# Two-layer streaming trunk: longer runs of equal products, both output projections in half blocks, one engine swap and a block of gates moved

## The chip, the cores and the metric

The kernel runs on one core of one Trainium2 chip. The time is device microseconds of one execution; the kernel before has a median of 1018.46 us over three runs (1017.2 to 1019.1). All durations inside the kernel are from the trace of one profiled execution.

## The reference

A batch of one, 256 frames, model width 2048, two layers, each h = h + Mixer(RMSNorm(h)), in float32. Cut to what matters:

```python
# layer A: gated delta rule, 16 heads of 128, chunks of 64 frames
proj = h @ w_in                                   # 2048 x 8224: q, k, v, z, a, b
qkv = silu(causal_depthwise_conv(proj[..., :6144], conv_w))
q, k = l2_norm(q) * 128 ** -0.5, l2_norm(k)
gc = cumsum(-exp(a_log) * softplus(a + dt_bias)); decay = exp(where(tril, gc_i - gc_j, -inf))
u, w = triangular_solve(I + tril(k_beta @ k.T * decay, -1), [v_beta, k_beta * exp(gc)])
# scan over the chunks: v_new = u - w @ state; o = q_dec @ state + (q k.T * decay) @ v_new
y = (rms_norm(o, out_norm_w) * silu(z)) @ w_out   # 2048 x 2048

# layer B: attention in a band of 9 chunks, 16 heads of 128
proj = h @ w_in                                   # 2048 x 8192: q, k, v, z
p = softmax(rms_norm(q) @ rms_norm(k).T * 128 ** -0.5 + bias[rel])
y = ((p @ v) * silu(z)) @ w_out                   # 2048 x 2048
```

## The kernel before, in words

Nearly all of TensorE's work is the four big projections. Their weights come from HBM in 320 chunks of 512 KB (tile `wt`, four buffers), each once. For each chunk ScalarE rounds it to a high part (`whi`, L199) and VectorE takes the rest as a low part (`wlo`, L200). The activations are split in the same way (`xb`, or `g` for the output projections, with an axis of two for the high and the low part), and a product is high x high + high x low + low x high. The sums are gathered in PSUM in tiles named `psp`; the small matmuls of the mixers use tiles named `pss`.

A chunk is used in one of three forms (`KINDS`, L260).
- features (L234): 512 weight columns, two k-tiles of 128 rows. Four times per k-tile three products of 256 columns: L237, L239, L240.
- half (L242): 256 weight columns, four k-tiles. For a k-tile and one of two column groups there is one long product of 512 columns (the high weights by both parts of the activations, L247) and one short one of 256 (the low weights by the high part, L250): a pair. Four long ones are followed by four short ones (`GROUP` = 2 k-tiles by 2 column groups). When such a block is done, its two sums are joined by a copy on ScalarE (L303) and an addition on VectorE (L304).
- tokens (L253): the activations are the stationary side; three products of 512 columns: L256, L257, L258.

`plan` lists the chunks in order. A full block is 8 chunks in the features or the tokens form (`CPB`), 4 in the half form (`CPH`). Behind the products of each k-tile, `chunk` calls `step`, which advances one of two queues of background work (`bgq`, `bg2`), generators that emit a piece at each `yield`. That is how the convolutions, the decays, the inversion, the recurrence and the attention get in between the products. The order in which the program is written so is then arranged per engine, and each engine works through its instructions in that order.

The places that the change touches:
- `decays` (L455 to L492). For four groups of heads, right-hand sides are written (`rhs`, L457; the high part on VectorE, the low part on GpSimd, L460), TensorE sums them with constant triangular and all-one matrices (L475), and ScalarE takes exponentials (L480, L481, L483).
- `inversion` (L596). ScalarE first gathers blocks in eight copies (L610); VectorE transposes them (L620); later there are 64 matmuls of 32x32 (L650), and more of that size (L670).
- The end of layer A's recurrence, for the last four heads: the last products L780 to L782, squares on ScalarE (L783), their sum on VectorE (L789, L790), a power on GpSimd (L792), the scaling (L798) and the gates (L714) on VectorE; then `gated(3)` (L812) transposes the result on TensorE (L818) and writes it in two parts (L822, L823). The output projection's products for the k-tiles 12 to 15 need it: `ready` (L726) steps the queues until it has been emitted, and `drain` emits all that is left.
- Layer A's output projection starts before that. Its first 1024 columns are two features accumulators. Six of the eight chunks of each (`CUT`, the k-tiles 0 to 11) come first, then a drain, then the last two of each. The other columns are four half blocks. `ha_small` (L857) adds the input, whose rows GpSimd's queue fetches (L869), and splits the result for layer B.
- Layer B's input projection computes the gates z first (four pairs of half blocks; `zb_small`, which also asks for the bias rows), then v, then k and q for four groups of heads. `attend` has four stages: scores, weights (exponentials, L1023), turned (transposes L1037, copied by ScalarE in L1039) and values (L1047, L1048), behind which the gates are multiplied on. The last projection is cut like that of layer A.

## Time and profile before

| | |
|---|---|
| median of three runs | 1018.46 us |
| profiled execution, its time | 1018.52 us |
| its span | 1016.8 us |
| TensorE (PE) busy | 1005.7 us, 99% |
| VectorE (DVE) busy | 695.4 us, 68% |
| ScalarE (ACT) busy | 523.0 us, 51% |
| GpSimd (POOL) busy | 80.0 us, 8% |
| share of TensorE in the chain of waits | 95% |
| DMA | 177.56 MB, mean 175 GB/s |

In the rows of the profile an instruction stands with its line, its engine, its operation, its output and inputs by tile name, its shape and a count. PEld is TensorE's loading of the stationary side. A bracket gives the idle time of the engine ahead of the instruction, and who ended it. A matmul's duration reaches into the next one, so that the pace is the distance between starts. The view by windows gives, for a stretch, the busy time of each engine with a count of instructions, the granted clock of TensorE as a share of full speed, the DMA share and the rate.

### The profile page before, as it was taken

The numbers are of one execution on the slowest core, as the hardware profiler recorded it, in microseconds if no ns is written. First come the engines' busy times: TensorE is split into PE (matmuls) and PEld (weight loads), VectorE is DVE, ScalarE is ACT, GpSimd is POOL, SyncE is SP. The second block draws the span as 40 slices with busy tenths as digits, with TensorE's granted clock in tenths as the row PEclk, the third lists the DMA queues.
The fourth block names the chain that finished last, engine by engine and source line by source line (L and its number), as shares of the span: only waits on it lengthen the run. The fifth ranks groups of instructions, "written<-read, shape, count | busy, mean of one in ns | idle before, by whom it ended". The sixth has DMA issues, their size and how long they took to land.

```text
span 1016.8 us, 15574 instructions
## 1 busy us (share of the span) xinstructions
PE 1005.7 (99%) x6090; PEld 879.1 (86%) x6090; DVE 695.4 (68%) x1113; ACT 523.0 (51%) x724; POOL 80.0 (8%) x91
## 2 busy tenths in 40 slices
PE   8999999999999999999999999999999999999998
PEld 7987888888788989899988888888888888889987
DVE  7888889996988687755866555444456665666554
ACT  8475765555446455444654444444445555555442
POOL 2004000113000001001000000000011010101000
PEclk9999999999999999999999999999999999999999
DMA  8664665554664445545756766666665555544472
GB/s 289 183 187 115 178 184 155 156 166 146 185 190 144 108 142 149 163 145 168 246 187 187 228 207 207 188 195 196 189 186 177 153 169 163 165 154 159 158 228 90
DMA packets 134185, 177.56 MB, mean 175 GB/s; under 512 B 7904, under 2 KB 90208, under 8 KB 134112
## 3 DMA queue, kind: packets, MB, share of 16 engines
q1 hardware_dynamic: 132672, 172.12, 56.8%
q0 software_dynamic: 1152, 4.19, 1.2%
q8 instruction: 47, 0.77, 0.3%
q10 hardware_dynamic: 288, 0.26, 0.1%
q14 instruction: 26, 0.21, 0.1%
HBM read 174.46 MB, written 2.10 MB: 174 GB/s over the span
## 4 chain that ended last, share of the span: by engine, by line
PE 95%; DVE 2%; ACT 1%; issue 1%; DMA 1%; SPq 0%; ACTq 0%
PE psp L247 26%; PE psp L250 13%; PE psp L257 11%; PE psp L258 11%; PE psp L256 11%; PE psp L240 4%; PE psp L237 4%; PE psp L239 4%; PE pss L560 2%; DVE wlo L200 1%; PE pss L757 1%; PE pss L992 1%; PE pss L1011 1%; PE pss L1047 1%; PE pss L247 1%
## 5 line engine op out<-in xcount | busy, mean ns | idle before, releaser
L200 DVE TENSOR_TENSOR wlo<-wt,whi 128x1024 fp32r<-128x1024 f32 (+1 forms) x322 | 393.9, 1225 | 246.3 <-ACT whi L199 237.1
L199 ACT CAST whi<-wt 128x1024 fp32r<-128x1024 f32 (+1 forms) x322 | 336.4, 1046 | 399.3 <-PE psp L247 155.8
L247 PE MATMUL psp<-xb,whi 128*128 128x512 f32 x960 | 267.3, 397 | 0.3 <-DVE ev L304 0.3
L257 PE MATMUL psp<-wlo,xb 128*128 128x512 f32 x512 | 201.3, 393 | 1.6 <-DVE wlo L200 1.6
L258 PE MATMUL psp<-whi,xb 128*128 128x512 f32 x512 | 201.7, 394 | 0.0
L256 PE MATMUL psp<-whi,xb 128*128 128x512 f32 x512 | 200.3, 391 | 0.0
L247 PEld LDWEIGHTS psp<-xb,whi 128*128 128x128 f32 x960 | 165.1, 190 | 22.2 <-PE psp L250 0.5
L250 PEld LDWEIGHTS psp<-xb,wlo 128*128 128x128 f32 x960 | 147.9, 190 | 19.7
L250 PE MATMUL psp<-xb,wlo 128*128 128x256 f32 x960 | 156.7, 283 | 0.0
L257 PEld LDWEIGHTS psp<-wlo,xb 128*128 128x128 f32 x512 | 96.2, 188 | 21.6 <-DVE wlo L200 2.0
L256 PEld LDWEIGHTS psp<-whi,xb 128*128 128x128 f32 x512 | 96.2, 188 | 19.9 <-ACT whi L199 0.3
L258 PEld LDWEIGHTS psp<-whi,xb 128*128 128x128 f32 x512 | 96.3, 188 | 19.1
L239 PE MATMUL psp<-g,whi 128*128 128x256 f32 x256 | 73.5, 287 | 0.0
L237 PE MATMUL psp<-g,whi 128*128 128x256 f32 x256 | 73.5, 287 | 0.0
L240 PE MATMUL psp<-g,wlo 128*128 128x256 f32 x256 | 72.9, 285 | 0.0
L503 DVE SCALAR_TENSOR_TENSOR cv<-raw,sm,cv 128x254 f32<-128x254 f32 (+2 forms) x144 | 62.1, 477 | 1.8 <-ACT cv L501 1.8
L247 PE MATMUL psp<-g,whi 128*128 128x512 f32 x224 | 61.2, 395 | 0.0
L239 PEld LDWEIGHTS psp<-g,whi 128*128 128x128 f32 x256 | 49.1, 192 | 0.2
L237 PEld LDWEIGHTS psp<-g,whi 128*128 128x128 f32 x256 | 49.1, 192 | 0.1
L240 PEld LDWEIGHTS psp<-g,wlo 128*128 128x128 f32 x256 | 49.1, 192 | 0.1
L247 PEld LDWEIGHTS psp<-g,whi 128*128 128x128 f32 x224 | 38.3, 189 | 5.1
L250 PEld LDWEIGHTS psp<-g,wlo 128*128 128x128 f32 x224 | 34.4, 189 | 4.7
(248 smaller groups left out, 995.3 us busy)
## 6 DMA issues: line engine op xcount, KB each, us to landing
wt<-in_b_w_in_dram SPq DMA_DIRECT2D x128, 512.0 KB, 3.7
wt<-in_a_w_in_dram SPq DMA_DIRECT2D x127, 512.0 KB, 3.9
wt<-in_a_w_out_dram SPq DMA_DIRECT2D x32, 512.0 KB, 3.9
wt<-in_b_w_out_dram SPq DMA_DIRECT2D x32, 512.0 KB, 3.6
dl<-in_xT_dram POOLq DMA_DIRECT2D x4, 512.0 KB, 5.7
dl<-in_relb_dram POOLq DMA_DIRECT2D x4, 512.0 KB, 5.3
g<-in_xT_dram SPq DMA_DIRECT2D x7, 256.0 KB, 5.2
out_dram<-cv SPq DMA_DIRECT2D x2, 512.0 KB, 3.7
```

The costliest lines, as they stand in the source:

```text
L199: act.copy(out=hi[:, js, cs], in_=wt[:, js, cs])
L200: dve.tensor_tensor(out=lo[:, js, cs], in0=wt[:, js, cs], in1=hi[:, js, cs].bitcast(F32), op=ALU.subtract)
L237: pe.matmul(ps, lhsT=hi[:, j, fs], rhs=xb[:, kt, 0, :], start=(kt == 0 and s % 2 == 0), stop=False, skip_group_check=True)
L239: pe.matmul(ps, lhsT=hi[:, j, fs], rhs=xb[:, kt, 1, :], start=False, stop=False, skip_group_check=True)
L240: pe.matmul(ps, lhsT=lo[:, j, fs], rhs=xb[:, kt, 0, :], start=False, stop=(kt == KT - 1), skip_group_check=True)
L247: pe.matmul(ps[s], lhsT=hi[:, j, s * P:(s + 1) * P], rhs=xb[:, ks[j], :, :], start=(ks[j] == 0), stop=False, skip_group_check=True)
L250: pe.matmul(ps[s][:, 0, :], lhsT=lo[:, j, s * P:(s + 1) * P], rhs=xb[:, ks[j], 0, :], start=False, stop=(ks[j] == KT - 1), skip_group_chec ...
L256: pe.matmul(ps, lhsT=xh, rhs=hi[:, j, :], start=(kt == 0), stop=False)
L257: pe.matmul(ps, lhsT=xh, rhs=lo[:, j, :], start=False, stop=False)
L258: pe.matmul(ps, lhsT=xl, rhs=hi[:, j, :], start=False, stop=(kt == KT - 1))
L503: dve.scalar_tensor_tensor(out=cv[:, i, s:], in0=raw[:, i, :T - s], scalar=conv_w(i0 + i, 3 - s), in1=cv[:, i, s:], op0=ALU.mult, op1=ALU.add)
L560: pe.matmul(dst, lhsT=kq[:, a, i, c:c + P], rhs=rhs, start=(n == 0), stop=(n == 2))
```

## The change

- In the half form a whole chunk is one group: eight long products (four k-tiles by two column groups), then eight short ones. Odd chunks start with the short ones, so that where two chunks meet, sixteen of a kind follow each other.
- Background work is advanced in smaller portions: `tick` counts a credit, in the tokens form after each of the two halves of a k-tile. The inversion yields more often. The third block of layer A's gates has the rate 2, not 1.
- The decays' low parts are written by ScalarE: 32 copies of 128x128 with a scale in place of eight products on GpSimd.
- Both output projections have eight half blocks. The first part is now two half blocks with three of four chunks each.
- In layer B the last group's gates (256 x 2 columns) are computed behind the last queries. The last four heads' attention results are kept (`late`) and gated when these gates are there (`late_gates`). The fourth request for bias rows goes behind the values' first block.

```diff
-    CUT = (3 * CPB) // 4
     CUTH = (3 * CPH) // 4
 
-    def cut_halves(w, col):
+    def cut_halves(w, col, n=6):
 
         p = []
         for c0, c1 in ((0, CUTH), (CUTH, CPH)):
             for j in range(2):
                 p += half(w, col + 256 * j, c0, c1)
-        return p + halves(w, col + 512, 6)
-
-    for c0, c1 in ((0, CUT), (CUT, CPB)):
-        for j in range(2):
-            plan += wide(a_w_out, 512 * j, c0, c1)
-    plan += halves(a_w_out, 1024, 4)
-    plan += cut_halves(b_w_in, 6144)
+        return p + halves(w, col + 512, n)
+
+    plan += cut_halves(a_w_out, 0)
+
+    plan += cut_halves(b_w_in, 6144, 4)
     for gi in range(4):
         plan += wide(b_w_in, 4096 + 512 * gi)
     for gi in range(4):
         for col in (2048, 0):
             plan += wide(b_w_in, col + 512 * gi)
-    for c0, c1 in ((0, CUT), (CUT, CPB)):
-        for j in range(2):
-            plan += wide(b_w_out, 512 * j, c0, c1)
-    plan += halves(b_w_out, 1024, 4)
+    plan += halves(b_w_in, 7680, 2)
+    plan += cut_halves(b_w_out, 0)
...
+    credit = [0.0]
+
+    def tick(n):
+
+        while now:
+            now.pop(0)()
+        credit[0] += n
+        while credit[0] >= 1:
+            credit[0] -= 1
+            step()
...
+    def features2(ps, hi, lo, ks, xb):
+
+
+        turns = (ks[0] // len(ks)) % 2
+        for n, long in enumerate((not turns, turns)):
+            for s in range(2):
+                for j, kt in enumerate(ks):
+                    w = (hi if long else lo)[:, j, s * P:(s + 1) * P]
+                    dst, x = (ps[s], xb[:, kt, :, :]) if long else (ps[s][:, 0, :], xb[:, kt, 0, :])
+                    pe.matmul(dst, lhsT=w, rhs=x, start=bool(long and kt == 0), stop=(n == 1 and kt == KT - 1),
+                              skip_group_check=True)
+                yield
...
         if kind == "half":
             ps = ps if isinstance(ps, list) else [ps[:, s] for s in range(2)]
-            for j in range(0, kc, GROUP):
-                js = range(j, j + GROUP)
-                if pre is not None:
-                    for jj in js:
-                        pre(ks[jj])
-                features2(ps, hi, lo, js, ks, xb)
-                step(rate)
+            if pre is not None:
+                pre(ks[-1])
+            for _ in features2(ps, hi, lo, ks, xb):
+                tick(rate / 2)
             return
         for j, kt in enumerate(ks):
             if pre is not None:
                 pre(kt)
             for s in range(ns):
                 f(ps[:, s], s, j, kt, hi, lo, xb)
-            step(rate)
+                tick(rate / ns)
...
-                for part, src in ((0, g_r), (1, gl_r)):
-                    (pool if part else dve).tensor_tensor(
-                        out=rbuf[:, gi % 2, 2 * half + part, :].rearrange("p (h c) -> p h c", h=4),
-                        in0=lt_f.unsqueeze(1).broadcast_to([P, 4, P]),
-                        in1=src[:, 4 * gi:4 * gi + 4, half].bitcast(F32).unsqueeze(2).broadcast_to([P, 4, P]),
-                        op=ALU.mult)
+                dve.tensor_tensor(
+                    out=rbuf[:, gi % 2, 2 * half, :].rearrange("p (h c) -> p h c", h=4),
+                    in0=lt_f.unsqueeze(1).broadcast_to([P, 4, P]),
+                    in1=g_r[:, 4 * gi:4 * gi + 4, half].bitcast(F32).unsqueeze(2).broadcast_to([P, 4, P]),
+                    op=ALU.mult)
+                for i in range(4):
+                    act.activation(out=rbuf[:, gi % 2, 2 * half + 1, i * P:(i + 1) * P], in_=lt_f, func=AF.Copy,
+                                   scale=gl_r[:, 4 * gi + i, half:half + 1].bitcast(F32))
...
                 act.copy(
                     out=stg[pr].rearrange("p (h t) c -> p h t c", t=2)[:, :, t, :],
                     in_=dl[pr, :, 0, T * t + 32 * b:T * t + 32 * b + 32])
-            yield 1
+                yield 1
...
+                if i == 7:
+                    yield 1
...
+                if i % 4 == 3 and i < 15:
+                    yield 1
...
-        bg2.append(za_small(gi, block("tokens", xb, 1 if gi == 2 else 2)))
+        bg2.append(za_small(gi, block("tokens", xb, 2)))
...
-
-    pa = [acc("features") for _ in range(2)]
-    for n in (CUT, CPB - CUT):
+    pa = [acc("half") for _ in range(2)]
+    for n in (CUTH, CPH - CUTH):
         for j in range(2):
-            if n != CUT and j == 0:
+            if n != CUTH and j == 0:
                 drain()
             for _ in range(n):
-                chunk("features", pa[j], gmem["b"], 2, ready(gmem))
-            if n != CUT:
-                a_done(j, pa[j], 4 * j, 4 * j + 4)
-    for j in range(4):
-        a_done(j + 2, block("half", gmem["b"], 2), 8 + 2 * j, 10 + 2 * j)
+                chunk("half", pa[j], gmem["b"], 2, ready(gmem))
+            if n != CUTH:
+                bgq.append(ha_small(pa[j], slice(2 * j, 2 * j + 2)))
+    for j in range(2, 8):
+        bgq.append(ha_small(block("half", gmem["b"], 2), slice(2 * j, 2 * j + 2)))
...
-    for j in (1, 2, 3):
+    for j in (1, 2):
...
+            if gi == 3:
+
+                act.copy(out=late[:, i, :], in_=ps[:, :T])
+                return
...
+    late = hmem["m"][:, 8192:9216].rearrange("p (h t) -> p h t", h=4)
+
+    def late_gates():
+        for i in range(0, 4, 2):
+            o, hs = late[:, i:i + 2, :], slice(12 + i, 14 + i)
+            dve.tensor_tensor(out=o, in0=o, in1=bmem["z"][:, hs, :], op=ALU.mult)
+            act.copy(out=gmem["h"][:, hs, :], in_=o)
+            dve.tensor_tensor(out=gmem["l"][:, hs, :], in0=o, in1=gmem["h"][:, hs, :].bitcast(F32), op=ALU.subtract)
+            gmem["done"] = 14 + i
             yield 1
...
+    bgq.append(zb_small(3, pair(xb)))
+    bgq.append(late_gates())
...
-    po = [acc("features") for _ in range(2)]
-    for n in (CUT, CPB - CUT):
+    po, evs = [acc("half") for _ in range(2)], [[], []]
+    for n in (CUTH, CPH - CUTH):
         for j in range(2):
-            if n != CUT and j == 0:
+            if n != CUTH and j == 0:
                 drain()
             for _ in range(n):
-                chunk("features", po[j], gmem["b"], 1, ready(gmem))
-            if n != CUT:
-                bgq.append(out_small(j, po[j]))
-    for n in range(4, 7):
+                chunk("half", po[j], gmem["b"], 1, ready(gmem))
+            if n != CUTH:
+                joined(po[j], evs[j])
+                bgq.append(out_half(j, evs[j]))
```

How this moves instructions is shown at three places, as each engine's order has them. The lines of the changed kernel are a little further on in each function than before.

ScalarE, at the start of the decays. Before, up to the second group's exponentials:

```order
L199 CAST whi<-wt 128x1024 x3
L480 ACT_TABLE_LOAD
L480 ACTIVATE dl<-pss 128x4x128
L483 ACTIVATE dl<-pss,tail 128x128 x4
L481 ACTIVATE dl<-pss 128x4x128
L199 CAST whi<-wt 128x1024
L303 COPY ev<-psp 128x512
L480 ACTIVATE dl<-pss 128x4x128
```

Now (L468 writes a low part, L485, L486 and L488 are the exponentials, L193 the cast, L306 the copy of an eviction):

```order
L193 CAST whi<-wt 128x1024 x2
L468 ACTIVATE tt<-kT,gl_r 128x128 x16
L193 CAST whi<-wt 128x1024
L468 ACTIVATE tt<-kT,gl_r 128x128 x4
L485 ACT_TABLE_LOAD
L485 ACTIVATE dl<-pss 128x4x128
L193 CAST whi<-wt 128x1024
L306 COPY ev<-psp 128x512
L488 ACTIVATE dl<-pss,tail 128x128 x4
L486 ACTIVATE dl<-pss 128x4x128
L468 ACTIVATE tt<-kT,gl_r 128x128 x4
L193 CAST whi<-wt 128x1024
```

Twenty copies stand ahead of the first exponential, the other twelve between the later ones.

TensorE, at the end of layer A's recurrence. Before, the last products of the recurrence, and the first transposes of the last gates behind 76 products of the output projection:

```order
L782 MATMUL pss<-dl 128x128
L239 MATMUL psp<-g,whi 128x256
L240 MATMUL psp<-g,wlo 128x256
L237 MATMUL psp<-g,whi 128x256
...
L239 MATMUL psp<-g,whi 128x256
L818 MATMUL pss<-ident,dl 128x128 x2
```

Now (L789 to L791 are the recurrence's last products, L827 the transposes, L255 both kinds of product in the half form):

```order
L255 MATMUL psp<-g,wlo 128x256 x2
L791 MATMUL pss<-dl 128x128
L789 MATMUL pss<-dl 128x128
L790 MATMUL pss<-dl 128x128
L791 MATMUL pss<-dl 128x128 x2
L789 MATMUL pss<-dl 128x128
L790 MATMUL pss<-dl 128x128
L791 MATMUL pss<-dl 128x128
L827 MATMUL pss<-ident,dl 128x128 x8
L255 MATMUL psp<-g,wlo 128x256 x16
```

The transposes follow the recurrence's last product at once.

TensorE, at the end of the last attention. Before, 25 products stood between the transposes of a head's weights and its product with the values:

```order
L1037 MATMUL pss<-ident,raw 128x128 x3
L240 MATMUL psp<-g,wlo 128x256
L237 MATMUL psp<-g,whi 128x256
...
L240 MATMUL psp<-g,wlo 128x256
L1047 MATMUL pss<-pT,kT 128x256
L1048 MATMUL pss<-pT,kT 128x128
```

Now (L1046 are the transposes, L1056 and L1057 the products with the values):

```order
L255 MATMUL psp<-g,wlo 128x256 x8
L1056 MATMUL pss<-pT,kT 128x256
L1057 MATMUL pss<-pT,kT 128x128
L1046 MATMUL pss<-ident,raw 128x128 x3
L1056 MATMUL pss<-pT,kT 128x256
L1057 MATMUL pss<-pT,kT 128x128
L255 MATMUL psp<-g,whi 128x512 x8
```

The last head's product with the values follows its transposes at once.

More of the change, by code (lines that the diff above doesn't have):

```diff
@@ L217, in tile_hybrid_trunk, with step @@
     turn = [0]
-    def step(n=1):
+    def step():
         while now:
             now.pop(0)()
-        for _ in range(n):
-            lanes = (bgq, bg2) if turn[0] else (bg2, bgq)
-            turn[0] ^= 1
-            for lane in lanes:
-                if advance(lane):
-                    break
+        lanes = (bgq, bg2) if turn[0] else (bg2, bgq)
+        turn[0] ^= 1
+        for lane in lanes:
+            if advance(lane):
+                break
+    credit = [0.0]
[6 more added lines that the diff above has]
+            step()
     def drain():
@@ L869, in ha_small @@
             nc.gpsimd.dma_start(out=hmem["h"][:, qs, :], in_=xv[:, qs, :])
[L870 to L873 removed]
+        ev = work.tile([P, 2, T], F32, name="ev", tag="ev")
+        act.copy(out=ev, in_=ps[:, :, 1, :])
         yield 1
[L875 to L880 removed]
+        if k0 in (0, 4):
+            dve.tensor_copy(out=hmem["h"][0:1, k0 + 8, 0:1], in_=ev[0:1, 0, 0:1])
+        dve.tensor_tensor(out=h, in0=ps[:, :, 0, :], in1=h, op=ALU.add)
+        dve.tensor_tensor(out=h, in0=h, in1=ev, op=ALU.add)
         yield 1
@@ L936, in zb_small, with bias_load @@
         yield 1
+    def bias_load(gi, after):
+        bias, hs = bmem["bias"], slice(4 * gi, 4 * gi + 4)
+        dve.tensor_copy(out=bias[0:1, 4 * gi, 0:1], in_=after)
+        nc.gpsimd.dma_start(out=bias[:, hs, :], in_=relb[:, hs, :])
+        pool.memset(bias[0:64, hs, 192:256], NEG)
     while "x" not in hmem:
```

40 lines of the change are left out of this document (8 added, 32 removed).

## The prediction

> **What bounds the kernel now.** The busy times and the chain of waits come first.
>
> ```profile
> span 1016.8 us, 15574 instructions
> PE 1005.7 (99%) x6090; PEld 879.1 (86%) x6090; DVE 695.4 (68%) x1113; ACT 523.0 (51%) x724; POOL 80.0 (8%) x91
> PE 95%; DVE 2%; ACT 1%; issue 1%; DMA 1%; SPq 0%; ACTq 0%
> ```
>
> TensorE is busy for 99% of the span and carries 95% of the chain. A change can therefore save time in two ways only: by fewer or shorter matmuls, or by removing one of TensorE's few waits. Work added to ScalarE or VectorE costs nothing until TensorE waits for it. The waits of TensorE are the next view (total, times, longest):
>
> ```profile
> PE pss L475 <- ACT dl L480: 1.8, 1, 1.8
> PE psp L257 <- DVE wlo L200: 1.6, 1, 1.6
> PE psp L240 <- DVE wlo L200: 1.0, 2, 0.8
> PE pss L670 <- issue: 0.7, 1, 0.7
> PE psp L247 <- DVE ev L304: 0.3, 1, 0.3
> ```
>
> These five sum to 5.4 us, and none of them lies in layer A's output projection or in layer B (the L240 one is at the start). So what can be won is small, and any new wait is a loss of its full length. The third view is the pace of the products, in TensorE's timeline:
>
> ```profile
> 300.04 1.09 PE L247 MATMUL psp<-xb,whi 128*128 128x512 f32 x4
> 300.97 0.63 PE L250 MATMUL psp<-xb,wlo 128*128 128x256 f32 x4
> 305.65 0.63 PE L247 MATMUL psp<-xb,whi 128*128 128x512 f32 x2
> ...
> 640.02 0.39 PE L256 MATMUL psp<-whi,xb 128*128 128x512 f32 x1
> 643.88 0.39 PE L258 MATMUL psp<-whi,xb 128*128 128x512 f32 x1
> ...
> 471.29 0.28 PE L239 MATMUL psp<-g,whi 128*128 128x256 f32 x1
> 474.53 0.28 PE L239 MATMUL psp<-g,whi 128*128 128x256 f32 x1
> ```
>
> The duration of a matmul overlaps the next one, so starts are compared. In half blocks, four rounds of four long and four short products take 305.65 - 300.04 = 5.61 us, which is 351 ns for a pair of one long and one short. The first four long ones of a round take 0.93 us, 232 ns each, and the short ones the rest, 118 ns each. Long products without short ones between (17 from 640.02 to 643.88) come every 227 ns. Products of 256 columns in the features form (27 from 471.29 to 474.53) come every 120 ns, and a pair's worth is three of them: 360 ns.
>
> **The products (edits one and two).** The first eight k-tiles of both output projections, 2 x 128 pairs, go from 360 to 351 ns: 256 x 9 ns = 2.4 us gained. That is sure as arithmetic of the two forms. Runs of eight, which join into sixteen of a kind where two chunks meet, may bring more: if only the first four long ones of a run take 232 ns and the rest 227, sixteen take 3.66 us; sixteen short ones, four at 118 and twelve at 120, take 1.91 us. Together that is 348 ns per pair, about 2.8 less than now. There are 960 + 224 half-block pairs in these two rows:
>
> ```profile
> L247 PE MATMUL psp<-xb,whi 128*128 128x512 f32 x960 | 267.3, 397 | 0.3 <-DVE ev L304 0.3
> L247 PE MATMUL psp<-g,whi 128*128 128x512 f32 x224 | 61.2, 395 | 0.0
> ```
>
> 1184 x 2.8 ns = 3.3 us, and the 256 new pairs get 0.7 more. No row shows a long run of this form, so the bounds of the whole are 2.4 and 6.4 us. I take -4.5, the middle. The further copies and adds that evict the new half blocks are hidden: ScalarE is busy half of the span.
>
> **The decays.** GpSimd's eight products of the low parts go, and ScalarE gets 32 copies of 128x128. What GpSimd did to VectorE, and the stall that came of it, is in the timeline:
>
> ```profile
> 82.40 5.45 POOL L460 TENSOR_TENSOR tt<-kT,gl_r 128x512 fp32r<-128x512 f32 x3
> 83.44 2.06 DVE L200 TENSOR_TENSOR wlo<-wt,whi 128x1024 fp32r<-128x1024 f32 x1
> 87.70 0.74 PE L475 MATMUL pss<-tt,ones_r 128*128 128x512 f32 x2 [1.77 <-ACT dl L480]
> 93.38 1.21 DVE L200 TENSOR_TENSOR wlo<-wt,whi 128x1024 fp32r<-128x1024 f32 x1
> ```
>
> While GpSimd works, VectorE's subtraction takes 2.06 us, afterwards 1.21. L475 waits for the right-hand sides that GpSimd writes (ScalarE, which the view names, had been idle, next fence). With GpSimd out of it I take this stall as gone: -2.2 us with the smaller one after it, bounds -2.2 and 0. What ScalarE pays:
>
> ```profile
> 87.05 0.60 ACT L480 ACTIVATE dl<-pss 128x512 f32<-128x512 f32 x1 [6.17 <-DVE tail L479]
> 95.30 0.60 ACT L480 ACTIVATE dl<-pss 128x512 f32<-128x512 f32 x1 [1.75 <-DVE tail L479]
> 99.23 0.60 ACT L480 ACTIVATE dl<-pss 128x512 f32<-128x512 f32 x1 [0.87 <-DVE tail L479]
> 99.72 1.13 ACT L483 ACTIVATE dl<-pss,tail 128x128 f32<-128x128 f32 x4
> 100.72 1.07 ACT L199 CAST whi<-wt 128x1024 fp32r<-128x1024 f32 x1
> 114.32 0.94 PE L247 MATMUL psp<-xb,whi 128*128 128x512 f32 x3 [0.33 <-DVE ev L304]
> ```
>
> Four 128x128 exponentials fill 100.72 - 99.72 = 1.00 us, so 32 copies fill 8.0 us. In the order sixteen of them stand in a row, with four more behind the next cast, ahead of the first exponential. ScalarE is idle 6.17 us there, but it then needs nearly every slot. Everything behind (the other exponentials, the copies of the convolutions, the evictions) comes later, and the last row shows that TensorE already waits for an eviction at 114. If the 6.17 us take all of it, the cost is 0; if only the 1.75 + 0.87 us among the exponentials do, it is 8.0 - 2.6 = 5.4 us. I take +2.5.
>
> **The steps that are spread.** The eight copies of the inversion's set-up get a yield each. In the timeline they are what stalls TensorE at 255:
>
> ```profile
> 249.39 5.03 ACT L610 COPY g<-dl 32x512 f32<-32x512 f32 x8
> 254.45 2.08 DVE L620 STREAM_TRANSPOSE g<-g 128x1024 f32<-128x1024 f32 x1 [3.13 <-ACT g L610]
> 256.45 1.19 DVE L200 TENSOR_TENSOR wlo<-wt,whi 128x1024 fp32r<-128x1024 f32 x1
> 257.69 0.50 PE L257 MATMUL psp<-wlo,xb 128*128 128x512 f32 x1 [1.64 <-DVE wlo L200]
> ```
>
> In the new order they still stand in one row of eight with no cast between, and one cast earlier than before; so do the 64 small products of 32x32. I count 0, with bounds of -1.6 (the stall goes) and +1.7 (it doubles).
>
> **The end of layer A's recurrence.** This is the largest term. The first part of the output projection covered this chain: two wide accumulators of six chunks, 288 products of 120 ns, 34.6 us. Now it is two half blocks of three chunks, 48 pairs of 0.35 us, 16.8 us. The order shows the consequence: between the last product of the recurrence (L782) and the transposes of the last gates (L818) there is no product left. The chain in between, from the timeline:
>
> ```profile
> 465.31 0.39 PE L782 MATMUL pss<-dl 128*128 128x128 f32 x2
> 465.74 0.60 ACT L783 ACTIVATE dl<-pss 128x512 f32<-128x512 f32 x1 [0.30 <-PE pss L782]
> 466.37 1.22 DVE L789 TENSOR_REDUCE so<-dl 128x8 f32<-128x1024 f32 x1 [1.07 <-ACT dl L783]
> 467.94 1.64 POOL L792 TENSOR_TENSOR ro<-so,nhalf 128x8 f32<-128x8 f32 x1 [25.66 <-DVE so L790]
> 469.88 1.28 DVE L798 TENSOR_TENSOR dl<-pss,ro 128x512 f32<-128x512 f32 x2
> 471.19 1.29 DVE L714 TENSOR_TENSOR dl<-dl,kT 128x512 f32<-128x512 f32 x2
> 476.60 1.41 DVE L823 SCALAR_TENSOR_TENSOR g<-pss,sm,g 128x512 fp32r<-128x512 f32 x2 [0.88 <-ACT g L822]
> ```
>
> L782 ends at 465.70. The first of the two L714 lands half-way, at 471.8: TensorE waits 6.1 us for it. Then come eight transposes, and the next products need what L822 and L823 make of them: L823's second instruction ends 1.4 us after its first begins, and part of this falls behind the transposes. I add 1.4: 7.5 us together. The bounds are 6.1 (all of the rest hidden) and 478.01 - 465.70 = 12.3 (the chain as late as it was before, when nothing waited for it).
>
> **The clock.** One stretch of before ran below full clock, in the view by windows (PE, PEld, DVE, ACT, POOL, then the granted clock):
>
> ```profile
> 84.00:88.00 4.00, 2.23 (x12) 1.62 (x11) 4.00 (x4) 0.95 (x3) 3.85 (x3) 1.00 0.66 178
> 325.80:329.20 3.40, 3.40 (x24) 2.85 (x15) 0.00 (x0) 3.31 (x6) 0.00 (x0) 0.50 0.50 144
> ```
>
> 3.40 us at half clock cost 1.7 us; they follow the tiny products and their 0.7 us stall. The 2 us stall at 86 left the clock at 1.00. The new idle time is about three times as long as any in this trace. The bounds are 0 (like the stall at 86) and 3.4 (two such stretches); I take one, +1.7. The Trainium skill, in TensorE: Matmul & The Clock Gate, Part 1 (What's actually happening), states that the clock halves after an idle window of about 3.4 us and comes back after a busy one of that length. By that rule the wait would bring such a stretch and the sum below would stand; by the row at 86 alone it would be 1.7 us less.
>
> **The end of layer B.** The last gates' block goes behind the queries, and the first part of the last projection shrinks as in layer A. The table load that this adds on ScalarE lies beside products. In the order the transposes of the last head's weights are followed at once by its product with the values, where 25 products of 0.12 us stood before, so TensorE waits for the copy between:
>
> ```profile
> 849.27 0.48 ACT L1039 COPY pT<-pss 128x384 f32<-128x384 f32 x1 [2.23 <-PE pss L1037]
> ```
>
> 0.48 us and the way there and back, about 0.8; and one eviction of the gates' block behind it, of the kind that cost 0.3 at 114, which I put at 0.7 because it queues behind that copy. Together +1.5, bounds 0.5 and 2.5.
>
> **The sum.** The profiled execution took 1018.52 us (span 1016.8), 0.06 above the median of the runs. 1018.5 - 4.5 - 2.2 + 2.5 + 0 + 7.5 + 1.7 + 1.5 = 1025.0 us.
>
> **The rivals.** (a) Faster: the cover holds. If the recurrence runs earlier against the products than in before, so that its chain ends while the last products of the first part still run, the wait at its end falls to 2 us or less, with no dip of the clock; then 1018.5 - 6.4 - 2.2 + 0 + 2 + 1.5 = 1013.4. For it: L782 in before was placed, not waited for, 28 us after the first part began. Against: the order has no product there, whatever the timing. It decides if that wait is below 4 us. (b) No change that can be told: the pace gives all 6.4, the decays cost nothing on ScalarE, the stall at 85 goes, and only the wait of 7.5 is left with some clock: 1018.5 - 6.4 - 2.2 + 7.5 + 1 = 1018.4. For it: each is a bound that rows allow. (c) Slower still, with ScalarE as the bound in the decays: 5.4 us there, the stall of 255 grows by 1.7, and the pace gives only 2.4: 1025.0 + 2.9 + 1.7 + 2.1 = 1031.7. For it: sixteen copies ahead of a cast that TensorE needs. (d) The change doesn't do what it says: runs of sixteen keep the pace of 351 ns, since each starts with slow long products, all else as forecast: 1025.0 + 2.1 = 1027.1; this is inside the forecast's own range.
>
> **How the numbers follow.** The forecast with (d) 0.60, its own range 1021 to 1029; (a) 0.16; (b) 0.14; (c) 0.10. The 8-in-10 range leaves out half of (a) and a part of (c): 1015.0 to 1030.0. About 0.2% (2 us) is what a measurement of this kernel can tell from no change. Faster: (a), 0.16; same: (b), 0.14; slower: the rest, 0.70.
>
> **What would show it.** The products' pace: a pair in 348 ns in half blocks. The decays: no wait at the first product with the ones, VectorE's subtraction at 1.2 throughout, ScalarE without idle time between 80 and 110, and a wait for an eviction behind it. The inversion: one wait for a low part at 250 to 260. The recurrence: a wait of 6 to 8 us for VectorE's last gates ahead of the transposes, and a granted clock of 0.5 behind it. I am wrong if that wait is under 4 us.

## The result

| | median us | runs us | ratio to before (95%) |
|---|---|---|---|
| before | 1017.83 | 1016.75 to 1019.10 | |
| changed | 1032.63 | 1028.72 to 1034.43 | 1.0142 (1.0119 to 1.0165) |

The changed kernel is 14.8 us slower, where 6.5 was forecast, and its median lies 2.6 us above the range. The profiled execution took 1034.43 us, span 1032.7, which is the slowest of the four; its mean granted clock is 0.987 where that of before is 0.998. (A fourth run of before, 1016.75 us, brings its median from 1018.46 to 1017.83.) The page of the changed kernel:

```profile
span 1032.7 us, 15151 instructions
PE 1009.1 (98%) x5834; PEld 873.2 (85%) x5834; DVE 694.3 (67%) x1121; ACT 539.0 (52%) x767; POOL 65.7 (6%) x83
PE 96%; DVE 1%; ACT 1%; issue 1%; DMA 1%; SPq 0%; POOL 0%; DVEq 0%; POOLq 0%
```

TensorE has 256 instructions fewer and is busy 3.4 us longer: a product at half clock takes longer (256 columns every 0.21 us at 13 us, every 0.12 at full clock). The waits of TensorE that the argument needs:

```profile
PE pss L827 <- DVE dl L723: 6.0, 1, 6.0
PE psp L255 <- DVE ev L307: 4.9, 4, 4.2
PE psp L255 <- DVE dl L885: 1.8, 1, 1.8
PE pss L679 <- issue: 1.6, 1, 1.6
PE psp L263 <- DVE wlo L194: 1.6, 1, 1.6
PE psp L241 <- ACT whi L193: 1.5, 1, 1.5
PE pss L1056 <- ACT pT L1048: 0.6, 1, 0.6
```

The first row is the wait ahead of the last gates' transposes; the second an eviction behind the decays; the third is for the input rows that are added to the first half blocks of the output projection, and was not in the sum. The wait for GpSimd at 85 us (the row of L475 in before) is gone, the one at 255 (here L263 for a low part) is the same to a tenth. The timeline at the three places, engines mixed:

```profile
79.30 4.80 ACT L468 ACTIVATE tt<-kT,gl_r 128x128 fp32r<-128x128 f32 x16 [0.28 <-DVE gl_r L453]
117.23 3.78 PE L255 MATMUL psp<-xb,whi 128*128 128x512 f32 x8 [4.17 <-DVE ev L307]
298.88 3.82 PE L255 MATMUL psp<-xb,whi 128*128 128x512 f32 x16
304.44 3.82 PE L255 MATMUL psp<-xb,whi 128*128 128x512 f32 x16
473.90 2.14 PE L827 MATMUL pss<-ident,dl 128*128 128x128 f32 x8 [5.97 <-DVE dl L723]
476.18 3.78 PE L255 MATMUL psp<-g,wlo 128*128 128x256 f32 x16
```

The products are as short as the upper bound of the forecast had them: from 298.88 to 304.44 there are sixteen pairs, 347.5 ns each. But the eight long products at 117 take 3.78 us where eight take 1.8, the eight transposes at 474 take 2.14 where they need 0.9, and the sixteen short products behind them 3.78 where the ones at 302 take 1.9. The view by windows says why (its seventh figure is the granted clock):

```profile
117.50:121.00 3.50, 3.50 (x9) 2.72 (x10) 3.50 (x10) 0.00 (x0) 0.00 (x0) 0.50 0.42 131
324.80:328.30 3.50, 3.50 (x16) 2.96 (x12) 1.19 (x4) 3.35 (x6) 0.00 (x0) 0.50 0.45 137
474.00:477.00 3.00, 2.86 (x12) 2.15 (x13) 1.28 (x3) 1.33 (x2) 0.31 (x1) 0.50 0.00 0
476.00:480.00 4.00, 3.86 (x18) 3.82 (x18) 1.41 (x2) 0.77 (x2) 1.78 (x2) 0.50 0.39 83
```

Read in windows of 0.1 us, the clock is at half for 27.5 us of the changed kernel's span (12.9 to 16.3, 115.3 to 122.2, 323.5 to 330.4 and 470.3 to 480.6 us). In before it is at half for 3.4 us, and for the last 1.5 us, behind TensorE's work. Some 6 of the 27.5 us are idle time, in which it costs nothing.

### The profile page after: what moved, and what is told of

Same layout as the page of the kernel before. It is cut to its first block, busy times and chain, and to the rows that moved or that the text cites. A ratio compares the mean times of both kernels' runs of the same rounds, so it can differ in the third digit from the quotient of the medians.

```text
span 1032.7 us, 15151 instructions
## 1 busy us (share of the span) xinstructions
PE 1009.1 (98%) x5834; PEld 873.2 (85%) x5834; DVE 694.3 (67%) x1121; ACT 539.0 (52%) x767; POOL 65.7 (6%) x83
## 4 chain that ended last, share of the span: by engine, by line
PE 96%; DVE 1%; ACT 1%; issue 1%; DMA 1%; SPq 0%; POOL 0%; DVEq 0%; POOLq 0%
PE psp L255 48%; PE psp L263 11%; PE psp L264 11%; PE psp L262 11%; PE pss L565 2%; PE pss L255 1%; PE psp L244 1%; PE pss L766 1%; PE psp L241 1%; PE psp L243 1%; PE pss L1001 1%; PE pss L1020 1%; PE pss L1056 1%; DMA g<-in_xT_dram 1%; PE pss L480 1%
## 5 line engine op out<-in xcount | busy, mean ns | idle before, releaser
L193 ACT CAST whi<-wt 128x1024 fp32r<-128x1024 f32 (+1 forms) x322 | 336.5, 1046 | 385.3 <-PE psp L255 183.0
L255 PE MATMUL psp<-xb,whi 128*128 128x512 f32 x960 | 239.9, 396 | 4.4 <-DVE ev L307 4.4
L255 PEld LDWEIGHTS psp<-xb,whi 128*128 128x128 f32 x960 | 176.5, 190 | 38.8 <-DVE ev L307 5.2
L263 PE MATMUL psp<-wlo,xb 128*128 128x512 f32 x512 | 200.9, 392 | 1.6 <-DVE wlo L194 1.6
L255 PE MATMUL psp<-xb,wlo 128*128 128x256 f32 x960 | 133.0, 287 | 0.0
L255 PEld LDWEIGHTS psp<-xb,wlo 128*128 128x128 f32 x960 | 127.8, 194 | 5.8
L255 PE MATMUL psp<-g,whi 128*128 128x512 f32 x480 | 116.6, 393 | 2.3 <-DVE dl L885 1.8
L263 PEld LDWEIGHTS psp<-wlo,xb 128*128 128x128 f32 x512 | 96.2, 188 | 21.6 <-DVE wlo L194 1.9
L255 PEld LDWEIGHTS psp<-g,whi 128*128 128x128 f32 x480 | 88.2, 189 | 20.1 <-ACT ev L880 2.2
L255 PEld LDWEIGHTS psp<-g,wlo 128*128 128x128 f32 x480 | 63.6, 196 | 3.0 <-ACT g L831 0.5
L255 PE MATMUL psp<-g,wlo 128*128 128x256 f32 x480 | 65.5, 288 | 0.1
L508 DVE SCALAR_TENSOR_TENSOR cv<-raw,sm,cv 128x255 f32<-128x255 f32 (+2 forms) x144 | 62.2, 474 | 2.5 <-ACT cv L506 2.3
L307 DVE TENSOR_TENSOR ev<-psp,ev 128x512 f32<-128x512 f32 x37 | 25.3, 683 | 0.7 <-ACT ev L306 0.6
L506 ACT ACTIVATE cv<-raw,sm 128x256 f32<-128x256 f32 x48 | 21.7, 501 | 6.5 <-DVE raw L322 6.1
L306 ACT COPY ev<-psp 128x512 f32<-128x512 f32 x37 | 21.4, 577 | 0.0
```

The source lines that it names most:

```text
L193: act.copy(out=hi[:, js, cs], in_=wt[:, js, cs])
L255: pe.matmul(dst, lhsT=w, rhs=x, start=bool(long and kt == 0), stop=(n == 1 and kt == KT - 1), skip_group_check=True)
L263: pe.matmul(ps, lhsT=xh, rhs=lo[:, j, :], start=False, stop=False)
L306: act.copy(out=ev, in_=ps[:, :, 1, :])
L307: dve.tensor_tensor(out=ev, in0=ps[:, :, 0, :], in1=ev, op=ALU.add)
L506: act.activation(out=cv[:, i, :], in_=raw[:, i, :], func=AF.Copy, scale=conv_w(i0 + i, 3))
```

## The experiments

All kernels are timed beside the one before, whose medians there are 1018.4 to 1019.0. "Half clock" below is read from short windows in each kernel's profiled run.

### Runs of eight alone

```diff
-            for j in range(0, kc, GROUP):
...
-                features2(ps, hi, lo, js, ks, xb)
-                step(rate)
...
+            for n, _ in enumerate(features2(ps, hi, lo, ks, xb)):
+                if n % 2:
+                    step(rate)
```

Here `features2` is that of the changed kernel, which yields four times per chunk.

> The kernel before with one edit: runs of eight long and eight short products, odd chunks the other way round; background work advanced twice per chunk, behind every second run. Theory (the runs bring the pace by which the changed kernel's products were shorter than forecast, about 346 to 348 ns per pair against 351): 1184 pairs x 3 to 5 ns, so 3.5 to 6 us less than before, 1012 to 1014.5 us, with no wait that before does not have. Rival (runs keep the pace, the shorter products of the changed kernel come from elsewhere): 1017 to 1019 us.

Measured: 1022.5 us, ratio 1.0028 (1.0014 to 1.0043). Both expectations are missed: the edit that shortens the products is slower by itself. The mean clock of its ten runs is 0.991 to 0.997, against 0.995 to 1.000 in nineteen of before, and the time goes with it: the run at 0.997 took 1018.0, those at 0.991 took 1022.5. The longest stretch at half clock lies at the inversion's small products. The timeline of this kernel, then its window and the same window of the kernel with the runs left out there (below):

```profile
318.57 2.07 PE L251 MATMUL psp<-xb,wlo 128*128 128x256 f32 x16
325.12 1.22 PE L251 MATMUL psp<-xb,whi 128*128 128x512 f32 x2
326.27 3.67 PE L685 MATMUL pss<-g,dl 64*64 64x64 f32 x32
329.87 4.21 PE L251 MATMUL psp<-xb,whi 128*128 128x512 f32 x9
334.01 1.91 PE L685 MATMUL pss<-g,dl 64*64 64x64 f32 x29
```

```profile
323.20:333.50 10.30, 9.37 (x88) 7.72 (x88) 4.86 (x10) 4.74 (x8) 0.00 (x0) 0.53 0.24 66
```

```profile
323.20:333.50 10.30, 10.24 (x276) 9.01 (x275) 6.11 (x11) 6.51 (x9) 0.00 (x0) 1.00 0.37 107
```

The last row of 32x32 products stands from 320.6 to 325.1 us, with a pause of 1.6 us in which TensorE waits for nothing that the profile shows (`issue`). Behind them come two large products, 64x64 ones (x32), nine large ones, and half clock lasts 10.3 us, which costs 5 us where before lost 1.7. The timeline of before at this place:

```profile
325.92 0.80 PE L247 MATMUL psp<-xb,whi 128*128 128x512 f32 x1
326.51 1.05 PE L250 MATMUL psp<-xb,wlo 128*128 128x256 f32 x4
327.37 1.91 PE L247 MATMUL psp<-xb,whi 128*128 128x512 f32 x4
329.07 0.70 PE L250 MATMUL psp<-xb,wlo 128*128 128x256 f32 x4
329.61 1.08 PE L247 MATMUL psp<-xb,whi 128*128 128x512 f32 x4
330.62 3.94 PE L685 MATMUL pss<-g,dl 64*64 64x64 f32 x64
```

In before the pause is 0.7 us, 17 large products follow ahead of the 64x64 ones, and the clock is back after 3.4 us. That the number of large products decides is not shown: in the changed kernel 17 stand there too, and half clock lasts 6.9 us. The pause differs more clearly. It is 1.6 to 2.7 us in the six profiles with runs of eight in layer A's values, and at most 1.0 us in seven of the eight others (1.7 in the eighth, the decays' low parts on ScalarE alone). Of the seven profiles with a long pause six have half clock there, of the seven with a short one only before. Why the pause grows stays open.

### Runs of eight, but not in layer A's values

```diff
-            for j in range(0, kc, GROUP):
-                js = range(j, j + GROUP)
+            group = GROUP if 88 <= i < 120 else kc
+            for j in range(0, kc, group):
+                js = range(j, j + group)
...
-                features2(ps, hi, lo, js, ks, xb)
-                step(rate)
+                for _ in features2(ps, hi, lo, js, ks, xb):
+                    step(rate)
```

Here i is the number of the chunk; `features2` gives four long and four short products for a group of two k-tiles, and two runs of eight for a group of four.

> The kernel before with the runs of eight in all half blocks but the eight of layer A's values, between which the inversion's small products stand. In the run with runs everywhere the clock stayed at half from 323 to 334 us, three times as long as before, with small products packed between two long runs. Theory (the runs of eight are shorter by 3 to 4 ns per pair, and it is this stretch that eats it): the stretch is 3.4 us as before, the gain of the other 1056 pairs is kept, 3 to 4 us less than before, 1014 to 1016 us. Rival (the lower mean clock of the runs of eight, 0.993 against 0.998, does not hang on this place): the mean clock stays at 0.994 or below and the time at 1019 us or more.

Measured: 1015.88 us, ratio 0.9974 (0.9964 to 0.9983), mean clock 0.997 to 1.000 in ten runs. The theory holds: what ate the gain was that place. Its count was off: layer A's values are 8 blocks of 32 pairs, so 928 pairs have runs of eight here, not 1056. 928 by 3.1 ns (350.6 less 347.5) are 2.9 us; 2.7 were measured.

### Layer A's output projection: taken back, and done alone

Taken back in the changed kernel:

```diff
-    plan += cut_halves(a_w_out, 0)
+    for c0, c1 in ((0, CUT), (CUT, CPB)):
+        for j in range(2):
+            plan += wide(a_w_out, 512 * j, c0, c1)
+    plan += halves(a_w_out, 1024, 4)
...
-    pa = [acc("half") for _ in range(2)]
+    pa = [acc("features") for _ in range(2)]
```

> The changed kernel with layer A's output projection as before: its first 1024 columns in the features form, first part of twelve chunks. Theory (the wait of 6.0 us at the end of the recurrence, the half clock behind it and the 1.8 us wait for the input rows all come from the short first part): about 11.7 us less and 1.6 more for 128 pairs in the slower form, so 10 us below the changed kernel, 1021 to 1024 us, with no wait above 0.5 us between 455 and 495 us. Rival (the chain of the recurrence is late in itself, by the finer steps): the wait at the transposes stays above 3 us and the time within 4 us of the changed kernel.

Measured: 1023.92 us, ratio 1.0052 (1.0035 to 1.0068), 8.7 us below the changed kernel. The waits at the transposes and for the input rows are not in its list, and the clock is full from 455 to 495 us. The other way round, in the kernel before with its runs of four:

```diff
-    for c0, c1 in ((0, CUT), (CUT, CPB)):
-        for j in range(2):
-            plan += wide(a_w_out, 512 * j, c0, c1)
-    plan += halves(a_w_out, 1024, 4)
+    plan += cut_halves(a_w_out, 0)
...
+    pa = [acc("half") for _ in range(2)]
```

> The kernel before with layer A's output projection in half blocks alone, in runs of four. Theory (the short first part uncovers the end of the recurrence): 128 pairs are 1.2 us shorter; a wait of about 6 us ahead of the transposes, 1.8 us for the input rows, 7 to 10 us at half clock (3.5 to 5 us): 9 to 12 us more than before, 1027 to 1031 us. Rival (the runs of sixteen put the recurrence's steps too late, and with runs of four there are products left beside the chain): the wait is under 3 us, the time within 4 us of before.

Measured: 1032.01 us, ratio 1.0129 (1.0114 to 1.0144). This one part costs 13.3 us, nearly as much as the whole change. Its waits there:

```profile
PE pss L816 <- DVE dl L712: 6.0, 1, 6.0
PE pss L755 <- DVE dl L765: 1.3, 1, 1.3
PE psp L245 <- ACT ev L869: 1.3, 1, 1.3
PE psp L245 <- DVE g L821: 0.9, 1, 0.9
PE pss L780 <- ACT dl L757: 0.7, 1, 0.7
```

They sum to 10.2 us. The clock is at half from 467.3 to 477.6 us, of which some 6 us are worked, 3 us lost. The rows of L755 and L780 are waits inside the recurrence: the short first part runs out of products a little earlier too.

### The idle time filled

Twenty products that nobody uses, in the changed kernel:

```diff
+NFILL = 20
...
             ps = ps_small()
+            if gi == 3 and p == 0:
+                busy = dl_work(3)
+                for n in range(NFILL):
+                    pe.matmul(ps[:, 0:P], lhsT=busy[:, 0, 0, :], rhs=busy[:, n % 4, 1, :], start=True, stop=True)
```

> The changed kernel with 20 products of 128x128 added whose sums nothing uses (the transposes behind them overwrite them). They stand between the recurrence's last product and the transposes of the last gates, read the squares that ScalarE has just written, and take about 20 x 0.22 = 4.4 us of the 6.0 us in which TensorE waits there. Theory (the half clock from 470 to 480 us comes from that idle time): the granted clock stays at 1.00 there, the transposes and products behind run at full pace, 4 to 5 us less, 1027.5 to 1029 us, and a wait of under 2 us is left. Rival (the clock falls for another cause, the pattern of long runs): it stays at half for 6 us or more, and the time is within 1 us of the changed kernel.

Measured: 1030.51 us, ratio 1.0119 (1.0104 to 1.0134), 2.1 below the changed kernel: between the two expectations. The timeline and the windows of this kernel (the trace has two entries for each of the added products):

```profile
465.84 3.85 PE L829 MATMUL pss<-dl 128*128 128x128 f32 x33
470.68 0.44 PE L832 MATMUL pss<-ident,dl 128*128 128x128 f32 x2 [1.00 <-DVE dl L724]
```

```profile
470.00:473.00 3.00, 1.70 (x10) 1.23 (x11) 1.64 (x3) 1.13 (x2) 0.20 (x1) 0.96 0.00 0
473.00:476.00 3.00, 3.00 (x16) 3.00 (x15) 1.00 (x2) 0.14 (x1) 1.59 (x2) 0.50 0.46 94
476.00:480.00 4.00, 3.94 (x18) 2.95 (x16) 0.29 (x1) 1.38 (x2) 0.00 (x0) 0.97 0.54 192
```

The transposes now run at full clock, and half clock lasts 3.4 us, not 10. So the idle time does bring the half clock. It isn't gone: waits of 1.00, 0.17 and 0.45 us are left, and one stretch stands behind them. Whether the transposes between these waits count as work for the clock is not shown. The wait for the input rows (1.8 us) is where it was.

### The decays' low parts: taken back, done alone, and split

Taken back in the changed kernel (GpSimd's instruction of before in place of the four copies):

> The changed kernel with the decays' low parts on GpSimd as before. Theory (the eviction that TensorE waits 4.2 us for at 113 us is late because 32 copies of together 9 us stand on ScalarE ahead of it; the half clock of 3.5 us follows from that wait): the wait at 113 falls below 1 us and the clock stays full there, 6 us less; the wait for GpSimd at 85 us comes back, 2.2 us more. 4 us below the changed kernel, 1027.5 to 1030 us. Rival (the runs of eight or the finer steps make the eviction late): the wait at 113 stays above 3 us, the time rises by 2 us.

Measured: 1032.95 us, ratio 1.0142 (1.0124 to 1.016): no difference. The wait at 113 us is gone, as the theory has it (the waits for L307 sum to 0.7 us, none above 0.3), and the 1.8 us at 85 are back. What the theory had not: half clock follows that wait here too (91.7 to 95.2 us), and the stretch behind the small products is 10.3 us in this profile, 6.9 in the changed kernel's. In all, TensorE works 20.4 us at half clock here and 21.2 there. Done alone in the kernel before:

```diff
-                for part, src in ((0, g_r), (1, gl_r)):
-                    (pool if part else dve).tensor_tensor(
...
+                for i in range(4):
+                    act.activation(out=rbuf[:, gi % 2, 2 * half + 1, i * P:(i + 1) * P], in_=lt_f, func=AF.Copy,
+                                   scale=gl_r[:, 4 * gi + i, half:half + 1].bitcast(F32))
```

> The kernel before with the decays' low parts on ScalarE alone (32 copies), products in runs of four as before. Theory (what the swap costs is what ScalarE has to do ahead of the convolutions' evictions): the wait at 85 us goes (2.2 us less), a wait for an eviction of about 4 us comes at 110 to 115 us, and it is long enough to bring 3.4 us of half clock each time (1.7 us): 3 to 4 us more than before, 1021 to 1023 us. Rival (the late eviction needs the runs of eight, whose steps come in larger lumps): the wait at 113 stays below 1 us and the time falls by 2 us.

Measured: 1024.43 us, ratio 1.0046 (1.0029 to 1.0062). The theory's wait is there without the runs of eight, with half clock behind it from 118.0 to 121.4 us. The time is 1.4 us above the theory's range; this profile has 6.8 us of half clock behind the small products too. The wait:

```profile
PE psp L247 <- DVE ev L304: 3.7, 1, 3.7
```

Last, in the kernel with runs of eight but in the values, only the first group's eight copies on ScalarE:

```diff
+                if gi:
+                    pool.tensor_tensor(
...
+                    continue
+                for i in range(4):
+                    act.activation(out=rbuf[:, gi % 2, 2 * half + 1, i * P:(i + 1) * P], in_=lt_f, func=AF.Copy,
+                                   scale=gl_r[:, 4 * gi + i, half:half + 1].bitcast(F32))
```

> The kernel with runs of eight but in layer A's values (the fastest so far), and only the first group's low parts on ScalarE (8 copies, 2.2 us), the other three groups' on GpSimd. Theory (the wait at 85 us is the first group's low parts on GpSimd, with VectorE slowed beside it; 8 copies fit in ScalarE's idle time there): the wait at 85 and the half clock that often follows it go, with no wait above 1 us at 113: 2 to 4 us below the kernel without this edit, 1012 to 1014 us. Rival (the second group's low parts then become what TensorE waits for, or the first copies delay the casts): the waits between 80 and 120 us sum to 2 us or more as before, and the time stays at 1015 to 1017 us.

Measured: 1015.27 us, ratio 0.9964 (0.9951 to 0.9977), mean clock 0.998 to 1.000 in five runs. Its waits between 80 and 120 us are

```profile
PE psp L252 <- DVE ev L310: 1.6, 1, 1.6
PE psp L252 <- DVE wlo L200: 1.2, 1, 1.2
```

Both signs of the rival hold: the waits sum to more than 2 us, and the time lies in its range. The median is the lowest of all, 0.6 us below the kernel without the edit, but the intervals of the two ratios (0.9964 to 0.9983 there) overlap, so a gain by this edit is not shown. Its profile, with more idle time than before but in two pieces, has no half clock ahead of the last microsecond.

### Layer B alone, and the finer steps alone

> The kernel before with layer B's edits alone: last gates behind the last queries, last projection in half blocks. 128 pairs in the shorter form save 128 x 9 ns = 1.2 us. Theory (the waits of 0.6 to 0.9, 0.6 and 0.4 us seen in the changed kernel at the end of the last attention belong to this edit): 1.9 us of waits, so 0.5 to 1 us more than before, within what can be told. Rival (the edit is a clean gain and its waits come from the runs): 1.2 us less, with no wait at the last head's product.

Measured: 1017.97 us, ratio 1.0004 (0.9990 to 1.0019). The theory's waits are there (0.6 us for the copy at the last head, gaps of 0.9 and 0.57 us where 0.1 is the pace) and take up the 1.2 us of shorter products. The time does not decide between the expectations: the interval has 1 inside.

> The kernel before with the finer steps alone: credit after each run of four, after each half of a k-tile, the inversion's further yields, the rate 2. Theory (the arrangement per engine puts the inversion's copies and small products together again): the wait at 255 us stays at 1.6 us or grows, and the time is within 2 us of before. Rival (the finer steps spread the copies, and the wait is gone): 2 us less.

Measured: 1020.28 us, ratio 1.0007 (0.9994 to 1.0021). As in the theory, the wait at 255 stays at 1.6 us; the eight copies still stand in a row, and no change of the time is shown.

### Two and three parts taken back

The output projection and the decays:

> The changed kernel with both of these undone: runs of eight, finer steps and layer B's edits are left. Theory (the two losses are separate and add): 14 us below the changed kernel, 1016 to 1020 us. Rival (they share a cause, such as a clock that stays lower for the whole run): the sum of the two gains is missed by more than 3 us.

Measured: 1021.88 us, ratio 1.0031 (1.0016 to 1.0046). That is 10.8 us below the changed kernel where 14 were expected, and 1.9 us above the theory's range. Its profile shows 6.9 us of half clock behind the small products. Taking the runs out of the values too:

> The changed kernel with three parts undone: layer A's output projection starts in the features form again, the decays' low parts are on GpSimd again, and layer A's values have runs of four. Left are the runs of eight elsewhere, the finer steps and layer B's edits. Theory (these three places hold all that makes the changed kernel slower than before): 1015 to 1018 us, the mean clock at 0.997 or above, no stretch at half clock over 4 us. Rival (there is a further loss in the finer steps or in layer B, of 2 us or more): 1019 to 1022 us, as with two parts undone.

Measured: 1016.12 us, ratio 0.9973 (0.9963 to 0.9984). With these three places as before, the changed kernel is 2.8 us faster than before and holds its clock (0.997 to 0.998 in ten runs): the loss is in these three. From the changed kernel on, taking back the output projection is worth 8.7 us, the decays behind it 2.0 and the runs in the values 5.8. Done alone in the kernel before, the three cost 13.3, 5.7 and 4.1 us, more than the change as a whole, so their costs do not add.

## Why the prediction was wrong in size

The direction, the likeliest cause and its place were right. By the steps of the sum:

| step | forecast us | found us | from |
|---|---|---|---|
| products | -4.5 (-6.4 to -2.4) | -6.9 | 1184 x 3.1 ns + 256 x 12.5 ns |
| wait at 85 | -2.2 | -2.2 | gone from the list of waits |
| ScalarE in the decays | +2.5 (0 to 5.4) | +4.6 | 4.9 us of waits for L307, 0.3 before |
| inversion's copies | 0 | 0 | 1.6 us in both |
| end of the recurrence | +7.5 (6.1 to 12.3) | +8.7 | 6.0, 0.9 of gaps, 1.8 for the input rows |
| clock behind it | +1.7 (0 to 3.4) | +3.3 | 6.6 worked us at half clock |
| end of layer B | +1.5 (0.5 to 2.5) | +1.5 | gaps beyond the pace |
| not in the sum: clock at 117 | | +2.4 | 4.8 worked us at half clock |
| not in the sum: small products | | +2.2 | 0.9 us more of issue, 6.0 us at half clock against 3.4 |
| not in the sum: the first 17 us | | +1.9 | the 51st large product starts at 16.49 us, in before at 14.54: 0.45 of waits, 1.5 of half clock |

The found column sums to 15.5, and the spans of the two profiles differ by 15.9. The changed kernel's profile is the slowest of its four runs, 1.8 us above their median.

**The recurrence's end** was right: TensorE waited 5.97 us where 6.1 was read from the rows of before, and taking the edit back or doing it alone moves 8.7 or 13.3 us. What the step missed is what is late next. The input rows are asked for only when the transposes' buffer is free, and their addition must free the sums; I had their request in the description of the kernel and gave it no price.

**The step that failed is the clock.** I priced one stretch of 3.4 us at one place: 1.7 us. The changed kernel's profile loses 8.5 us more than before to half clock, in four places (3.3, 2.4, 1.3 and 1.5 us). The rows of before gave one stretch behind the small products and none behind two waits of 2 us, and I took that as what such waits do. The runs show that the same wait does so in some executions and not in others. Behind the wait at 85 us, a gap of 2.1 to 2.4 us, six of the nine profiles that have it show half clock; behind that at 255, as long, two of fourteen. The kernel before itself runs at a mean clock between 0.995 and 1.000, and takes 1016.3 to 1017.0 us at 1.000 and 1020.3 to 1021.1 at 0.995; my one profile of it was at 0.998. Waits of 3.7 us and more had half clock behind them in every profile, for 3.4 to 10 us. So a new wait of that length costs its length and 1.5 to 3.3 us more. Most of what lies between the forecast and the result is this: 2.4 us at 117, 1.6 more at 474, 1.3 at 325, 1.5 at the start. The last of these is not the work of the order, which is the same for the first 12 us on each engine before and after; seven of the fourteen profiles have that stretch.

The traces show what decides. In each profile the stretches begin on a grid of 3.413 us: those of the changed kernel, at 12.9, 115.3, 323.5 and 470.3 us, lie 30, 61 and 43 steps apart. Where the grid lies differs from profile to profile. The wait at 85 us falls into one step in the profile with the output projection alone in half blocks (first two rows), and is divided between two steps in before (last two; the second figure is TensorE's busy time, the seventh the clock):

```profile
85.03:88.44 3.41, 1.64 (x9) 1.08 (x9) 3.41 (x4) 1.04 (x4) 3.17 (x2) 1.00 0.78 205
88.44:91.85 3.41, 3.41 (x12) 2.83 (x11) 3.41 (x7) 3.41 (x8) 0.62 (x1) 0.50 0.28 99
83.46:86.87 3.41, 2.48 (x14) 1.78 (x12) 3.41 (x3) 0.00 (x0) 3.41 (x3) 1.00 0.54 158
86.87:90.28 3.41, 2.58 (x13) 2.23 (x14) 3.41 (x8) 3.23 (x8) 1.51 (x2) 1.00 0.51 150
```

With the grid laid through one stretch of each of the 13 profiles that have one, all 14 steps at full clock in which TensorE is busy for under 1.6 us are followed by half clock, 10 of 17 with 1.6 to 1.9 us, and none of some 3500 with more. Steps with many 32x32 products are the exception: six of them, busy for 1.8 to 2.7 us, are followed by half clock too.

The Trainium skill, in TensorE: Matmul & The Clock Gate, Part 1 (What's actually happening), gives a free-running window of about 3.4 us and half rate after an idle one. The lengths of the stretches agree (3.4, 6.9, 10.3 us, and 0.50 in every window inside), and a free-running window fits the grid; but the traces show half clock behind gaps of 2.1 us too, less than a window.

**The decays.** The mechanism was right, shown from both sides: the wait is 3.7 us when the edit stands alone, and gone when it is taken back. ScalarE had 32 copies of 0.29 to 0.32 us in a row, 9.5 us in all and not 8.0, and too little idle time among the exponentials; the upper bound was nearer. In time the edit costs 5.7 us alone, 2.0 with the output projection taken back and nothing in the changed kernel, where half clock came elsewhere instead.

**The products** came out at their upper bound: 347.5 ns per pair where 348 was worked out from the settled paces. But the runs have a cost that no step named: at the inversion's small products they bring more half clock. With runs of eight everywhere the kernel is 4.1 us slower than before, with runs of eight but in the values 2.7 us faster. So the place is shown; by what means the runs do it there, a longer pause among the 32x32 products or the order behind them, is not.

**The rivals.** (a), a cover that holds, fell with the wait of 6 us. (b), gains that cancel, fell though the pace gave all and the wait at 85 went: ScalarE cost 4.6 us where it had nothing, and the clock 8.5 where it had 1. (c), ScalarE as the bound in the decays, gave 1031.7 and is nearest in time, but mostly for another reason: the decays cost 4.6 of its 5.4 us, but the wait at 255 did not grow and the pace was not missed. (d) fell: the pace was reached.

## What to carry to other kernels

Where TensorE is busy 99% of the span, price a wait as its length and the half clock behind it. In these traces that came always when a wait left TensorE busy for under 1.6 us of a step of 3.4 us, so waits of 3.7 us and more always brought it, and waits of 2 us sometimes. Look also at where small products stand. Work that covers a long chain has to be counted in microseconds against that chain before it's made shorter. And the order in which background work is let through is part of a change to the products' grouping: runs of eight were worth 2.7 us only with one stretch of the program left out of them.

## What was not expected of the hardware

Half clock comes in stretches of 3.4 us or two or three times that, behind idle gaps of 2 us in some executions and not in others, by where the gap lies on the grid of 3.413 us. 32x32 products with a pause of 0.7 us among them were enough in the profile of before. With 64x64 products among the large ones half clock lasted 10.3 us though TensorE was busy for 10.0 of them. Idle time in two pieces of 1.2 and 1.6 us, in the split decays, left the clock at 1.00 in the profile. Why small products count for less than their busy time is not shown.
